# Four more heads' queries and 14 instead of 10 blocks of activations as products of weight parts, with low parts by GpSimd

## The chip, the cores and the metric

The kernel runs on one core of one Trainium2 chip. The metric is the device time of one execution in microseconds (us), median of several runs. Before the change it is 2325.83 us (2325.72 to 2327.22, 3 runs).

## The reference

Two transformer blocks run one after the other on 256 tokens of width 1024, all in float32. The first has two layers, and each ends in a PEER feed-forward, the part that the change touches:

```python
def peer_ffn(x, w_q, sub_keys, u, v):
    """PEER: 8 retrieval heads, product keys, top-16 single-neuron experts per head."""
    ...
    q = (xt @ w_q).reshape(T, PEER_HEADS, 2, PEER_HALF)
    s = jnp.einsum('thcd,hcnd->thcn', q, sub_keys).astype(jnp.float32)
    s1, i1 = lax.top_k(s[:, :, 0], K)
    s2, i2 = lax.top_k(s[:, :, 1], K)
    cand_s = (s1[..., :, None] + s2[..., None, :]).reshape(T, PEER_HEADS, K * K)
    ...
    top_s, top_pos = lax.top_k(cand_s, K)
    ...
    gates = jax.nn.softmax(top_s, axis=-1).astype(x.dtype)
    ...
        act = jax.nn.gelu(jnp.einsum('thkd,td->thk', ub, xb), approximate=False)
```

Each token gets 16 experts per head out of 16384, by two lists of 128 keys. An expert's activation is gelu(u . x), and the result is the sum of v over the chosen experts, times gate and activation.

## The kernel before, in words

The kernel (class Kernel) keeps the activations x in SBUF and their transpose in two parts: xh, the high part in the format float32r, and xl, the rest. Weights come from HBM in loads of 1 MB ([128, 2048], line 248, all issued by SP) and each half of 1024 columns, a block, is cut in the same way by split (line 251): ScalarE writes the high part wh (line 257), VectorE the low part wl = w - wh (line 259). A product is then three: high by high, high by low, low by high (mm3, lines 283 to 288). col_plain (line 345) is the other form: plain float32 without parts, which the profile shows as two products for each one of the code. wh and wl have four buffers each, so a fifth block can't be cut before TensorE has used the first.

peer (line 663) runs once per layer. It computes the activations of all 16384 experts, 128 expert groups of 128, and weighs them with a gate matrix that is zero where an expert isn't chosen. It has three stages.

1. The retrieval (lines 716 to 879). queries (line 758) multiplies x by the query weights of a head, two blocks; scores (line 774) multiplies by the keys; select (line 784) finds the 16 best on VectorE by rounds of MAX8, FIND_INDEX8 and MATCH_REPLACE8, adds the candidates (line 793) and picks again; experts (line 804) works out the chosen experts of four heads on VectorE, once after head 4 and once at the end; line 864 takes the exponential of the gates on ScalarE, after line 863 on VectorE. The results are transposed on TensorE (line 873). Heads 2 and 3 use parts (QSPLIT), the others plain float32. Beside this, u_until (line 700) computes activations ahead, a pair of blocks from one load at a time; in the retrieval in plain float32 from xr, the unsplit transpose: 2 groups after head 6, 4 after head 7 (UA = 2), 10 before the last experts (UB = 10).
2. The gate stage (lines 886 to 942): 16 steps of gate_matrix, in which VectorE builds one-hot matrices A and B (lines 892 to 900) and TensorE multiplies them (line 905); u_until continues between the steps up to 38 of the 40 groups that are computed ahead (LEAD - REST), now with parts.
3. The weighing (lines 943 to 963): the rest of the activations, and the output weights v of all experts.

The program is written in the order of a loop, but a scheduler places the instructions of each engine; each engine then runs its own queue in order and waits on semaphores.

Of the kernel before, what the change touches and what calls it, by code (L numbers as in the profile page):

```python
# [9 lines left out]
F32 = mybir.dt.float32  # L10
# [10 lines left out]
T = 256  # L21
# [8 lines left out]
QSPLIT = (2, 3)  # L30
# [4 lines left out]
# ---------------------------------------------------------------- host layout  # L35
def _plan(widths):
    """Blocks of the given widths, packed into loads of at most GW columns."""
    groups, off = [], 0
    cur = []
    for w in widths:  # L40
        if cur and sum(cur) + w > GW:
            groups.append((off, cur))
            off += P * sum(cur)
            cur = []
        cur.append(w)
    groups.append((off, cur))
    return groups, off + P * sum(cur)
# [13 lines left out]
def _cols(w, n0, n=P):  # L61
    """[K, N] -> [128, K/128 * n]: contraction on partitions, chunk by chunk."""
    k = w.shape[0]
    return w[:, n0:n0 + n].reshape(k // P, P, n).transpose(1, 0, 2).reshape(P, -1)
# [33 lines left out]
def layout(i):  # L98
# [24 lines left out]
    # MLA  # L123
# [12 lines left out]
    # second block  # L136
# [62 lines left out]
# ---------------------------------------------------------------- kernel  # L199
class Kernel:  # L200
# [23 lines left out]
    # -------- weights  # L224
    def places(self, *more):
        """Where loads go from here, besides their own two places: pools, or tiles that are idle."""
# [24 lines left out]
    def split(self, src, w):  # L251
# [7 lines left out]
        nc.vector.tensor_tensor(l[:, :w], src, h[:, :w].bitcast(F32), op=ALU.subtract)  # L259
        return h, l  # L260

    def stream(self, name, width=None, split=True, fine=0):
        """The blocks of a weight, cut into pieces of the given width, as (high, low) or as they are. The first
        loads may be cut into blocks."""
# [18 lines left out]
    def mm3(self, out, a, b, first, last):  # L283
        """out += a.T @ b, both as (high, low)."""
# [5 lines left out]
    def banks(self, nt, nb):  # L290
        """[nt][nb] psum banks of 512 columns."""
        return [[self.mm.tile([P, 512], F32, name="row", tag="mm") for _ in range(nb)] for _ in range(nt)]

    def rows_steps(self, ps, blocks, xT, ks, width=D, hold=0, first=True, last=True, pieces=None):
        """ps[t][n] += x[t, ks] @ W[ks, n], W in blocks of whole rows. The last blocks, as many as held, are taken
        for one token tile after the other, so that the first is done early; the second then by pieces of
        columns, if they are given, with a psum for each."""
# [37 lines left out]
    def col_product(self, out, h, l, xT, nk, c0=0):  # L335
        """out[n, t] = W[:, n].T @ x.T, W as chunks of 128 columns."""
# [5 lines left out]
    def col_plain(self, out, w, x, nk):  # L342
        """The same in plain float32, which needs no parts."""
# [3 lines left out]
    # -------- transposes  # L347
    def turn(self, src, nk, c0=0):
        """x[t, k] of a token tile -> x.T in psum, 4 blocks of 128 in a bank."""
# [9 lines left out]
    def parts(self, banks, t, xT, gain=None, raw=None):  # L359
        """x.T as (high, low), times a gain per k; also as it is if raw is given."""  # L360
# [21 lines left out]
    # -------- norms  # L382
    def bcast(self, ap, n):
        """One row to all partitions."""
# [4 lines left out]
    def table(self, func, after=None):  # L389
        """Brings in the activation table of a function ahead of its use, once the last weight parts (or another  # L390
        [128, 1]) are there."""
# [8 lines left out]
    def ln_residual(self, ps, gb, t):  # L400
        """x = layer_norm(ALPHA * x + ps), one token tile."""
# [16 lines left out]
    def load_gb(self, l, j, pool=None):  # L418
        """Gain and bias of a layer norm, to all partitions."""
# [7 lines left out]
    # -------- log sigmoid of z  # L427
    def log_sigmoid(self, pool, out, z, shape):
# [9 lines left out]
        # what rounding took from 1 + e, over 1 + e to the first order  # L438
# [6 lines left out]
    # -------- mLSTM layer  # L445
    def mlstm(self):
# [3 lines left out]
        with ExitStack() as ctx:  # L450
# [43 lines left out]
            def gates():  # L494
# [13 lines left out]
                # lf in two parts, of which the first sums exactly; B and a in two parts too  # L508
# [89 lines left out]
            def normalise(g):  # L598
                """hs of four heads: y = hs / den, layer norm of y (but for its gain), times the output gate."""
# [9 lines left out]
                for t in range(2):  # L609
# [4 lines left out]
                    # sigmoid(z) = (1 + tanh(z / 2)) / 2  # L614
# [3 lines left out]
            # the output gate, four heads at a time, between the heads' products  # L618
# [33 lines left out]
    def ln_end(self, ps, gb, steps):  # L652
        """The rest of the products for the second token tile, over the layer norm of the first."""
# [8 lines left out]
    # -------- PEER  # L662
    def peer(self, l, ps, gb, banks):
        """ps, gb: psum of the layer before and its norm, which comes first; banks: x.T of its first token tile."""
# [3 lines left out]
        LEAD, KEEP, REST, HALF, UA, UB = 40, 8, 2, 64, 2, 10  # L668
        with ExitStack() as ctx:
            pools = [ctx.enter_context(tc.tile_pool(name=f"pe{j}", bufs=1)) for j in range(4)]  # L670
            pool = pools[3]
            # x waits in DRAM, its place takes loads
            xd = self.dram.tile([P, 2, D], F32, name=f"xd{l}")
            # gate matrices (64 i2 at a time) and activations ahead of their use, one [128, T] slot each
# [25 lines left out]
            def u_until(n, xr=None):  # L700
                """activations of the experts of two i2 at a time."""
                while nu[0] < min(n, P):
# [3 lines left out]
                    for j in range(2):  # L706
                        w = raw[:, j * BW:(j + 1) * BW]
                        if xr is not None:
                            self.col_plain(ps[:, j, :], w, xr, 8)
                        else:  # L710
                            self.col_product(ps[:, j, :], *self.split(w, BW), xT, 8)
# [4 lines left out]
            # retrieval  # L716
            with ExitStack() as c2:
# [4 lines left out]
                def carve(shape):  # L722
                    """float32 scratch in the slots of the first gate matrix."""
# [17 lines left out]
                # places for the first activations past those that come with the retrieval  # L741
# [11 lines left out]
                # The k-th best pair (a, b) of two sorted lists has (a + 1)(b + 1) <= k + 1, and every pair that  # L753
                # dominates it comes before it, so 64 of the 256 pairs hold the best 16, in the same order.
# [3 lines left out]
                def queries(hd, t=None):  # L758
                    """queries of a head, for one token tile or both."""
# [1190 lines left out]
```

## Time and profile before

| | |
|---|---|
| median of 3 runs | 2325.83 us (2325.72 to 2327.22) |
| profiled execution, span from first to last instruction | 2325.0 us |
| TensorE busy | 2284.3 us, 98% |
| VectorE busy | 1597.1 us, 69% |
| ScalarE busy | 1154.6 us, 50% |
| GpSimd busy | 17.2 us, 1% |
| retrieval of the first layer, from the first plain query product to the last transposes | 130.4 to 234.5 us |
| the same of the second layer ends at | 1188.3 us |

The profile names TensorE PE, VectorE DVE, ScalarE ACT, GpSimd POOL and SyncE SP; PEld is TensorE's weight load. A share over the whole span is an average over stages that have different limits, so a stage is read from the busy time in its own stretch and from the wait that ends last in it. The chain that ended last lies on TensorE for the most part; the profile's own list of it gives PE 46% of the span, DVE 2% and ACT 1%. The profiled execution lies within 0.04% of the median.

### The profile page before, as it was taken

How to read it: one execution, taken by the hardware profiler on the slowest of the kernel's cores; microseconds unless marked ns; L12 is line 12 of the kernel's file. 1: busy time of each engine (PE TensorE's matmuls, PEld its weight loads, DVE VectorE, ACT ScalarE, POOL GpSimd, SP SyncE). 2: the span in 40 equal slices, each digit the busy share in tenths (PEclk: the TensorE clock that was granted, in tenths of full speed). 3: DMA queues.
4: the chain of work that ended last, by engine and by line, in shares of the span. 5: the costliest groups of instructions: out<-in, count | busy, mean ns of one | idle time of the engine just before them, and what ended most of it. 6: DMA issues, size and time to landing. Idle time of an engine off the chain costs nothing. (4 is left out here: it accounts for less than half of the span.)

```text
span 2325.0 us, 38721 instructions
## 1 busy us (share of the span) xinstructions
PE 2284.3 (98%) x15802; PEld 2042.5 (88%) x15802; DVE 1597.1 (69%) x2959; ACT 1154.6 (50%) x1773; POOL 17.2 (1%) x41
## 2 busy tenths in 40 slices
PE   8999999999999999999999999999999999999998
PEld 7788998899999999887989889999999988778997
DVE  5789887677555555775998867765555567876555
ACT  5522554555444444574145555554444456466445
POOL 0000000000000000000000000000000000100000
PEclk9999999999999999999999999999999999999999
DMA  7352445545555655444334555455565556516451
GB/s 259 109 218 91 164 146 199 181 165 180 175 188 183 251 187 184 164 170 149 144 130 162 175 188 172 173 177 186 181 247 193 182 204 224 159 37 235 173 190 73
DMA packets 63519, 405.03 MB, mean 174 GB/s; under 512 B 9081, under 2 KB 12006, under 8 KB 17006
## 3 DMA queue, kind: packets, MB, share of 16 engines
q1 hardware_dynamic: 62462, 401.81, 49.2%
q8 instruction: 124, 2.03, 0.4%
q0 software_dynamic: 256, 0.52, 0.1%
q14 instruction: 53, 0.43, 0.1%
q10 hardware_dynamic: 624, 0.23, 0.0%
HBM read 398.48 MB, written 3.54 MB: 173 GB/s over the span
## 5 line engine op out<-in xcount | busy, mean ns | idle before, releaser
L259 DVE TENSOR_TENSOR wl<-raw,wh 128x1024 fp32r<-128x1024 f32 (+2 forms) x519 | 628.1, 1214 | 380.3 <-ACT wh L257 379.2
L257 ACT ACTIVATE wh<-raw 128x1024 fp32r<-128x1024 f32 (+2 forms) x519 | 542.0, 1050 | 476.9 <-PE pu L287 243.7
L286 PE MATMUL pu<-xh,wh 128*128 128x256 f32 x1888 | 537.8, 285 | 0.0
L287 PE MATMUL pu<-xl,wh 128*128 128x256 f32 x1888 | 535.6, 284 | 0.0
L288 PE MATMUL pu<-xh,wl 128*128 128x256 f32 x1888 | 535.4, 284 | 0.0
L286 PE MATMUL row<-wh,whi 128*128 128x512 f32 x1024 | 402.2, 393 | 0.0
L287 PE MATMUL row<-wl,whi 128*128 128x512 f32 x1024 | 399.0, 390 | 0.0
L288 PE MATMUL row<-wh,wlo 128*128 128x512 f32 x1024 | 398.7, 389 | 0.0
L286 PEld LDWEIGHTS pu<-xh,wh 128*128 128x128 f32 x1888 | 363.7, 193 | 3.4
L287 PEld LDWEIGHTS pu<-xl,wh 128*128 128x128 f32 x1888 | 363.5, 193 | 3.4
L288 PEld LDWEIGHTS pu<-xh,wl 128*128 128x128 f32 x1888 | 363.4, 193 | 0.0
L259 DVE TENSOR_TENSOR wl<-x,wh 128x1024 fp32r<-128x1024 f32 x156 | 191.1, 1225 | 133.0 <-ACT wh L257 133.0
L257 ACT ACTIVATE wh<-x 128x1024 fp32r<-128x1024 f32 x156 | 165.0, 1058 | 178.5 <-PE pu L287 126.2
L288 PEld LDWEIGHTS row<-wh,wlo 128*128 128x128 f32 x1024 | 192.2, 188 | 40.8
L286 PEld LDWEIGHTS row<-wh,whi 128*128 128x128 f32 x1024 | 192.6, 188 | 37.3
L287 PEld LDWEIGHTS row<-wl,whi 128*128 128x128 f32 x1024 | 192.6, 188 | 36.7
L924 ACT ACTIVATE whi<-store 128x512 fp32r<-128x512 f32 x128 | 81.1, 634 | 177.1 <-PE row L287 174.3
L925 DVE TENSOR_TENSOR wlo<-store,whi 128x512 fp32r<-128x512 f32 x128 | 88.5, 693 | 74.3 <-ACT whi L924 72.9
L287 PE MATMUL pgu<-xl,wh 128*128 128x256 f32 x352 | 99.7, 283 | 0.0
L288 PE MATMUL pgu<-xh,wl 128*128 128x256 f32 x352 | 99.6, 283 | 0.0
L286 PE MATMUL pgu<-xh,wh 128*128 128x256 f32 x352 | 99.5, 283 | 0.0
L286 PE MATMUL row<-wh,xh 128*128 128x512 f32 (+3 forms) x232 | 87.8, 380 | 1.7 <-ACT xh L370 1.5
(544 smaller groups left out, 3305.7 us busy)
## 6 DMA issues: line engine op xcount, KB each, us to landing
raw<-in_v_dram SPq DMA_DIRECT2D x88, 1024.0 KB, 4.9
raw<-in_u_dram SPq DMA_DIRECT2D x84, 1024.0 KB, 4.9
x<-in_v_dram SPq DMA_DIRECT2D x40, 1024.0 KB, 4.9
x<-in_u_dram SPq DMA_DIRECT2D x38, 1024.0 KB, 4.9
raw<-in_fgu_dram SPq DMA_DIRECT2D x22, 1024.0 KB, 4.8
raw<-in_pg_dram SPq DMA_DIRECT2D x12, 1024.0 KB, 5.4
raw<-in_fdn_dram SPq DMA_DIRECT2D x11, 1024.0 KB, 4.9
store<-in_pq_dram SPq DMA_DIRECT2D x10, 1024.0 KB, 7.3
```

Source lines behind the costliest of these rows:

```text
L257: nc.scalar.activation(h[:, :w], src, AF.Copy)
L259: nc.vector.tensor_tensor(l[:, :w], src, h[:, :w].bitcast(F32), op=ALU.subtract)
L286: mm(out, lhsT=a[0], rhs=b[0], start=first, stop=False)
L287: mm(out, lhsT=a[0], rhs=b[1], start=False, stop=False)
L288: mm(out, lhsT=a[1], rhs=b[0], start=False, stop=last)
L924: nc.scalar.activation(wh, w, AF.Copy)
L925: v.tensor_tensor(wl, w, wh.bitcast(F32), op=ALU.subtract)
```

## The change

Three things change in peer, and one helper. QSPLIT names heads 4 to 7 as well, so that their query weights are cut into parts. The activations in the retrieval are computed from parts, not in plain float32. UA goes from 2 to 3 and UB from 10 to 14, so that 7 pairs of blocks, not 5, are computed in the retrieval; since the gate stage continues up to the same 38 groups, it has 12 pairs, not 14. And split takes an engine for the low part: GpSimd for heads 4 to 7 and the activations of the retrieval, VectorE elsewhere. Comments and docstrings are gone, too, which moves line numbers by one or two.

```diff
-QSPLIT = (2, 3)
+QSPLIT = (2, 3, 4, 5, 6, 7)
...
-    def split(self, src, w):
+    def split(self, src, w, low=None):
...
-        nc.vector.tensor_tensor(l[:, :w], src, h[:, :w].bitcast(F32), op=ALU.subtract)
+        (low or nc.vector).tensor_tensor(l[:, :w], src, h[:, :w].bitcast(F32), op=ALU.subtract)
...
-        LEAD, KEEP, REST, HALF, UA, UB = 40, 8, 2, 64, 2, 10
+        LEAD, KEEP, REST, HALF, UA, UB = 40, 8, 2, 64, 3, 14
...
-            def u_until(n, xr=None):
+            def u_until(n, low=None):
...
-                        if xr is not None:
-                            self.col_plain(ps[:, j, :], w, xr, 8)
-                        else:
-                            self.col_product(ps[:, j, :], *self.split(w, BW), xT, 8)
+                        self.col_product(ps[:, j, :], *self.split(w, BW, low), xT, 8)
...
-                            wq[hd] = [self.split(w, BW) for w in wq[hd]]
+                            wq[hd] = [self.split(w, BW, None if hd < 4 else nc.gpsimd) for w in wq[hd]]
...
-                        u_until(UA * (hd - 5), xr)
+                        u_until(UA * (hd - 5), nc.gpsimd)
...
-                u_until(UB, xr)
+                u_until(UB, nc.gpsimd)
```

Two places show how the queues change. GpSimd's queue, from the first layer's mixer to the second block, before (E is the mixer's mask, kcT belongs to the second block):

```order
L582 AFFINE_SELECT E_641<-E_641 128x128 x2
L582 AFFINE_SELECT E_642<-E_642 128x128 x2
L1482 MEMSET kcT 128x30
L1786 MEMSET gqd 128x1024
L1546 MEMSET rep 128x512
```

and after the change:

```order
L583 AFFINE_SELECT E_641<-E_641 128x128 x2
L583 AFFINE_SELECT E_642<-E_642 128x128 x2
L260 TENSOR_TENSOR wl<-raw,wh 128x1024 x4
L260 TENSOR_TENSOR wl<-store_1267,wh 128x1024 x6
L260 TENSOR_TENSOR wl<-raw,wh 128x1024 x4
L260 TENSOR_TENSOR wl<-store_1267,wh 128x1024 x6
L260 TENSOR_TENSOR wl<-raw,wh 128x1024 x6
L260 TENSOR_TENSOR wl<-store_11305,wh 128x1024 x6
L260 TENSOR_TENSOR wl<-raw,wh 128x1024 x4
L260 TENSOR_TENSOR wl<-store_11305,wh 128x1024 x6
L260 TENSOR_TENSOR wl<-raw,wh 128x1024 x2
L1480 MEMSET kcT 128x30
```

There are 44 new subtractions, 22 in each layer, in a stretch where the queue was empty; raw and store are places of loads.

ScalarE's queue at the end of the first retrieval, before (pu is a product of activations, pS the scores of a head, line 864 the exponential of the gates):

```order
L713 ACTIVATE store_1267<-pu 128x512
L782 ACTIVATE store_1265<-pS_1994 128x512
L713 ACTIVATE store_1267<-pu 128x512
L864 ACT_TABLE_LOAD
L864 ACTIVATE store_1266<-store_1266 128x256
L257 ACTIVATE wh<-raw 128x1024 x2
L713 ACT_TABLE_LOAD
L713 ACTIVATE store_1267<-pu 128x512
L257 ACTIVATE wh<-raw 128x1024 x2
L713 ACTIVATE store_1267<-pu 128x512 x2
```

and after the change:

```order
L258 ACTIVATE wh<-store_1267 128x1024 x2
L711 ACTIVATE store_1267<-pu 128x512
L258 ACTIVATE wh<-store_1267 128x1024
L862 ACT_TABLE_LOAD
L862 ACTIVATE store_1266<-store_1266 128x256
L258 ACTIVATE wh<-store_1267 128x1024
L711 ACT_TABLE_LOAD
L711 ACTIVATE store_1267<-pu 128x512
L258 ACTIVATE wh<-raw 128x1024 x2
L711 ACTIVATE store_1267<-pu 128x512
```

High parts of the retrieval's own activations now stand on both sides of the exponential: 19 of the 22 before it, three behind it (the next high parts of raw belong to the last pair, and the ones after those to the gate stage).

## Rows read from the trace of the kernel before

**Rows 1.** The busy table: busy us (share of the span) and instructions.
```profile
PE 2284.3 (98%) x15802; PEld 2042.5 (88%) x15802; DVE 1597.1 (69%) x2959; ACT 1154.6 (50%) x1773; POOL 17.2 (1%) x41
```
**Rows 2.** Busy us by stretch; columns as in the first line.
```profile
core 0: us, PE busy (x) PEld busy (x) DVE busy (x) ACT busy (x) POOL busy (x), PEclk, DMA share, GB/s
148.00:184.00 36.00, 36.00 (x228) 33.52 (x227) 35.14 (x245) 7.02 (x12) 0.00 (x0) 1.00 0.50 193
...
216.00:235.00 19.00, 12.83 (x61) 10.88 (x60) 18.86 (x73) 7.80 (x11) 0.00 (x0) 0.94 0.15 53
...
235.00:245.00 10.00, 10.00 (x92) 9.96 (x91) 8.00 (x10) 4.17 (x8) 0.00 (x0) 0.77 0.48 198
...
245.00:265.00 20.00, 20.00 (x240) 19.87 (x239) 17.58 (x22) 10.79 (x22) 0.00 (x0) 1.00 0.47 159
...
265.50:272.27 6.77, 6.77 (x82) 6.73 (x81) 5.39 (x7) 3.70 (x8) 0.00 (x0) 1.00 0.45 157
```
**Rows 3.** Timeline, PE, retrieval ends: start us, duration us, [idle before <-releaser].
```profile
234.46 0.90 PE L873 MATMUL pT<-ident,store 128*128 128x128 f32 x3 [5.58 <-DVE store L836]
...
1188.30 0.53 PE L873 MATMUL pT<-ident,store 128*128 128x128 f32 x2 [4.45 <-DVE store L836]
```
**Rows 4.** Timeline, PE: one head as parts, one in plain float32.
```profile
147.59 0.36 PE L286 MATMUL pq<-xh,wh 128*128 128x256 f32 x1
...
153.41 1.06 PE L779 MATMUL pS<-store 128*128 128x128 f32 x8
...
168.75 7.07 PE L345 MATMUL pq<-store,raw 128*128 128x256 f32 x32
175.66 0.61 PE L779 MATMUL pS<-store 128*128 128x128 f32 x4
```
**Rows 5.** Groups of POOL: line, operation, count | busy us, mean ns | idle before.
```profile
L582 POOL TENSOR_SCALAR_AFFINE_SELECT E<-E 128x128 f32<-128x128 f32 x16 | 4.4, 294 | 82.6 <-DVE E L580 82.6
...
L1786 POOL MEMSET gqd<- 128x1024 f32 x1 | 1.0, 952 | 0.0
```
**Rows 6.** Timeline, DVE and POOL, in the second block.
```profile
1979.59 0.48 DVE L1450 SCALAR_TENSOR_TENSOR cacc<-hp,t_cvw,cacc 128x256 f32<-128x256 f32 x1
1979.82 1.04 POOL L1518 TENSOR_TENSOR flat<-dupk,t_cposk 128x240 f32<-128x240 f32 x1 [4.26 <-issue]
...
1980.18 0.95 DVE L1450 SCALAR_TENSOR_TENSOR cacc<-hp,t_cvw,cacc 128x256 f32<-128x256 f32 x1
...
1982.39 0.41 DVE L440 TENSOR_TENSOR ls_d<-ls_d,ls_e 128x256 f32<-128x256 f32 x1
1982.72 1.86 DVE L1450 SCALAR_TENSOR_TENSOR cacc<-hp,t_cvw,cacc 128x256 f32<-128x256 f32 x1
1982.88 0.74 POOL L1518 TENSOR_TENSOR flat<-dupk,t_cposk 128x240 f32<-128x240 f32 x1
1983.57 1.60 POOL L1518 TENSOR_TENSOR flat<-dupv,t_cposv 128x240 f32<-128x240 f32 x2
1984.51 0.94 DVE L442 TENSOR_TENSOR ls_u<-ls_u,ls_d 128x256 f32<-128x256 f32 x1
```
**Rows 7.** Timeline, DVE and POOL, some 20 us later.
```profile
2002.88 1.73 POOL L1801 TENSOR_SCALAR_AFFINE_SELECT gAT<-gAT 128x512 f32<-128x512 f32 x1 [17.71 <-ACT gAT L1800]
2002.90 1.22 DVE L259 TENSOR_TENSOR wl<-raw,wh 128x1024 fp32r<-128x1024 f32 x1
...
2004.93 0.63 POOL L1801 TENSOR_SCALAR_AFFINE_SELECT gAT<-gAT 128x512 f32<-128x512 f32 x1
```
**Rows 8.** Groups of DVE, 148 to 234 us: columns as in rows 5.
```profile
L829 DVE TENSOR_TENSOR oh<-kh,jm 128x1024 f16<-128x1024 f16 x8 | 5.4, 692 | 0.0
...
L793 DVE TENSOR_TENSOR cand<-store 128x32 f32<-128x32 f32 x16 | 2.8, 173 | 0.0
```
**Rows 9.** Timeline, ACT, end of the first retrieval.
```profile
218.42 0.42 ACT L864 ACTIVATE store<-store 128x256 f32<-128x256 f32 x1 [9.46 <-DVE store L863]
218.74 1.99 ACT L257 ACTIVATE wh<-raw 128x1024 fp32r<-128x1024 f32 x2
```

## The prediction

> **What bounds the kernel now.** I read four views. The busy table first [rows 1]: TensorE is busy for 98% of the span, GpSimd for 1%, and GpSimd has 41 instructions in all. Then busy time by stretch [rows 2], for the first of the two retrievals (148 to 235 us) and the gate matrices behind it (245 to 265 us). Two regimes show. In the retrieval VectorE has no hole (35.14 of 36.00 us, then 18.86 of 19.00), while TensorE runs out of work near its end (12.83 of 19.00). In the gate stage it is the other way: TensorE 20.00 of 20.00, VectorE 17.58. The third view, TensorE's waits, names the end of the retrieval [rows 3]: the transposes of line 873 wait 5.58 us for VectorE's last write of line 836, and 4.45 us in the second layer. So the retrieval ends when VectorE's selection ends; every product in it is filler. What TensorE saves there buys nothing by itself. It buys something only as work taken out of the TensorE-bound gate stage. The fourth view is the timeline around the few GpSimd operations that read SBUF beside VectorE [rows 6, 7].
>
> **TensorE's share.** Two blocks in plain float32 take 175.66 - 168.75 = 6.91 us from the first product to what follows; two blocks as three products of parts take 153.41 - 147.59 = 5.82 us [rows 4]. Per layer four heads and five pairs of activations change form: 9 x 1.09 = 9.8 us less. Two more pairs come in (14 instead of 10 blocks): 2 x 5.82 = 11.6 us more. TensorE has 1.8 us more to do in the retrieval, inside its 5.58 us (second layer 4.45) of waiting: price nothing while VectorE ends last.
>
> Those two pairs leave the gate stage. A step there with a pair takes 6.77 us of TensorE and 5.39 of VectorE [rows 2]; now three steps in four have one instead of seven in eight. A step without a pair needs 6.77 - 5.82 = 0.95 of TensorE and, two low parts of 1.22 less [rows 7], 2.95 of VectorE. Four steps: 3 x 6.77 + 0.95 = 21.3 against 3 x 5.39 + 2.95 = 19.1. TensorE still ends last, so all 11.6 us per layer come off, 23.3 us in both. Their two loads of 1 MB per layer move ahead on SP's queue too; the DMA share around the retrieval's end is 0.15 [rows 2], so I cost that at nothing.
>
> **ScalarE.** Twenty-two high parts per layer join a queue that is busy 7.02 of 36 and 7.80 of 19 us [rows 2]; at 1.0 us each (1.99 for two, [rows 9]) there is room. But order counts. The exponential of the gates waits 9.46 us for VectorE's line 863 [rows 9]; in the changed order the high part of the 20th block stands behind it, and with it the last three low parts on GpSimd. If VectorE keeps its time, that is at 218.4 us, TensorE stops for some 2 us, and its slack covers that. If VectorE is late, TensorE is late with it.
>
> **GpSimd, the unknown price.** No row has a subtraction of 128x1024 there. Bounds: the memset of 128x1024, which reads nothing, took 0.95 us; an addition of 128x240 with two inputs took 0.73, which scaled in full is 3.12 us [rows 5, 6]. The addition is the nearest. The selects took 0.29 us for 128 elements and 0.63 for 512 [rows 5, 7], which puts a fixed part at 0.29 - 0.34 / 3 = 0.18; so 0.18 + (0.73 - 0.18) x 1024 / 240 = 2.53 us, an estimate and my value. TensorE wants a block each 2.91 us, so 2.53 keeps up; 3.12 would not quite. GpSimd's queue holds nothing else there (0.00 us busy, [rows 2]), so nothing of before comes to stand behind the new operations.
>
> **What GpSimd does to VectorE.** This decides. Where GpSimd reads SBUF, VectorE's operations with two SBUF inputs stand still [rows 6]. The fused multiply-add of line 1450 takes 0.48 us alone; it took 0.95 when GpSimd's addition of 1979.82 ran, and 1.86 when two additions (1982.88, 1983.57) came one behind the other: it let both pass. The addition of line 442, 0.41 for its like at line 440, took 0.94 beside the third. These three GpSimd operations (0.74 and 1.60 for two) cost VectorE 1.38 + 0.53 = 1.9 us. The reverse is there too: beside a low part on VectorE (1.22 us) a GpSimd select took 1.73 instead of 0.63 [rows 7]. Whoever started first had its way.
>
> The Trainium skill says this as a rule ("SBUF — State Buffer", section "Who interferes with whom"): VectorE's instructions with two SBUF inputs and GpSimd's that read SBUF share an exclusive read interface, and the later one blocks until the earlier has ended. The trace agrees (0.48 became 1.86 us). It speaks against this change; without it the sum would be the second rival's.
>
> VectorE's operations are short (most 0.17 to 0.69 us, [rows 8]) and GpSimd's 2.53 long, so nearly all waiting falls on VectorE. Count it, per layer, for 22 GpSimd operations:
> 1. Selections of heads 0 to 4. Maxima and index searches have one input; only the four candidate additions of a head have two, in two places, so ten encounters. GpSimd works 2 x 2.53 us per head of 6.73 (5.82 + 0.9 for the scores, [rows 4]), a share of 0.75, with 1.27 us left on average: up to 10 x 0.95 = 9.5. The second place of a head comes close behind the first, which often just waited one out, so I take two thirds: 6.
> 2. The experts of heads 0 to 3: almost only two-input work. The four buffers of parts let GpSimd run four blocks ahead of TensorE; 12 low parts are done before and the 20th stands behind the exponential, so seven fall here. Each costs its length less what VectorE's running operation still needs, 2.3 us: 16.
> 3. The experts of heads 4 to 7: the last three, behind the exponential: 7.
>
> Sum 29 us per layer. The retrieval ends 29 later, the gate stage is 11.6 shorter: 17.4 per layer, 35 in both. The span (2325.0) and the median (2325.8) are 0.8 us apart, so 2326 + 35 = **2361 us**. With 0.95 us per GpSimd operation the same count gives 1.3 + 10 x 0.85 = 9.8 per layer and 2322; with 3.12 it gives 11 + 29.5 = 40.5 and 2384, and some 8 more over both layers if GpSimd is then also too slow for TensorE: 2392. TensorE's clock dropped over its wait (granted 0.77 in 235 to 245 us, [rows 2]); that start is paid in both kernels.
>
> The skill also has a time for the operation ("GPSIMD Engine Reference", section 3.1: 4497 ns for a float32 addition of 2048 elements); half of it, an estimate of 2.25 us, would make the sum about 2354. No run here shows that size.
>
> **Rivals.**
> - *GpSimd does the waiting* (2302 us). If VectorE's dense short operations hold GpSimd off, or a large GpSimd operation lets go in between, VectorE keeps its time and 23.3 us come off. For it: in rows 7 GpSimd was the one that waited, and TensorE has slack for it. Against: in rows 6 GpSimd's second addition went ahead of a VectorE operation that already waited.
> - *The waiting is shared* (2332 us): half of 29 is 14.5 per layer, less 11.6, twice. The balance lies at 11.6 us per layer, at about 1.1 us per GpSimd operation.
> - *One-input operations wait as well* (2414 us): then all 22 count, 22 x 2.53 = 55.7, less 11.6, twice 44. For it: nothing shows maxima or index searches beside GpSimd. Against: in rows 6 only two-input operations are stretched.
> - *The change doesn't do what it says*: if the new products starve, TensorE gains nothing in the retrieval, but it has slack there; this joins the forecast's upper end.
>
> **How the numbers follow.** Forecast 0.71 (its own range 2335 to 2392), shared waiting 0.09, GpSimd waits 0.15, one-input operations wait 0.05. A range of 2322 to 2392 leaves out the last two. A measurement of this kernel can tell about 0.2% (4.7 us) from no change. Faster: the 0.15 and a little of the low end, 0.17; same 0.05; slower 0.78.
>
> **What would show it.** Right: in the retrieval, candidate additions and the experts' operations of up to 2.5 us and more on VectorE with GpSimd's subtractions under them; the transposes of line 871 near 263 us, not 234; TensorE idle for some 20 us ahead of the block behind the exponential; two-block groups at 5.82 us; GpSimd busy for 44 x 2.53 = 111 us more. Wrong: VectorE's operations at their old lengths and GpSimd's stretched instead (second reading: the first rival); maxima longer than 0.3 us (the third); GpSimd's subtraction near 1 us or above 3.

## The result, and the profile after

The changed kernel takes 2355.84 us (median of 4 runs, 2355.57 to 2356.48) beside 2325.84 us for the kernel before (2325.72 to 2327.22): a ratio of 1.0128, 95% interval 1.0114 to 1.0143, so 30.0 us slower. The forecast was 2361, with a range of 2322 to 2392. The profiled execution has a span of 2353.9 us, 28.9 more than before, so the traces can be set side by side.

The busy table after the change, which answers to [rows 1]:

```profile
PE 2269.8 (96%) x16090; PEld 2041.9 (87%) x16090; DVE 1644.2 (70%) x2951; ACT 1187.0 (50%) x1809; POOL 125.3 (5%) x85
```

TensorE has 14.5 us less to do, GpSimd 108.1 us more, and VectorE, which lost eight low parts, is busy for 47.1 us more with 8 instructions fewer. Its operations became longer, not more.

Busy time by stretch, with the columns of [rows 2]:

```profile
148.00:184.00 36.00, 35.31 (x298) 35.11 (x297) 35.80 (x216) 16.56 (x22) 24.25 (x10) 1.00 0.64 241
184.00:216.00 32.00, 32.00 (x271) 32.00 (x270) 31.90 (x88) 14.77 (x17) 22.15 (x9) 1.00 0.29 100
216.00:240.00 24.00, 4.11 (x35) 3.90 (x33) 23.97 (x173) 1.03 (x2) 0.00 (x0) 0.64 0.00 0
240.00:255.00 15.00, 11.25 (x73) 10.72 (x73) 14.86 (x32) 8.50 (x11) 7.69 (x3) 0.78 0.20 70
```

VectorE still has no hole. From 184 to 216 it got through 88 instructions, while GpSimd worked 22.15 us; from 216 to 240, with GpSimd at 0.00, it got through 173 in a shorter stretch (the operations of the two stretches differ, so this is a hint and no measure). TensorE stands almost still there (4.11 of 24.00), where before it was short of work only for the last 6 us.

TensorE's longest waits, and where they lie in the first layer, answer to [rows 3]:

```profile
PE pu L287 <- ACT wh L258: 40.6, 2, 20.3
PE pT L871 <- DVE store L834: 10.8, 4, 3.8
```

```profile
240.38 0.58 PE L287 MATMUL pu<-xh,wh 128*128 128x256 f32 x1 [20.28 <-ACT wh L258]
259.40 0.90 PE L871 MATMUL pT<-ident,store 128*128 128x128 f32 x3 [3.75 <-DVE store L834]
```

ScalarE's queue tells why the first of these waits for a high part (beside [rows 9], where the same exponential began at 218.42):

```profile
238.97 0.42 ACT L862 ACTIVATE store<-store 128x256 f32<-128x256 f32 x1 [28.05 <-DVE store L861]
```

The exponential waits for VectorE, the 20th block's high part stands behind it, and TensorE waits for that. The last transposes of the first retrieval begin at 259.40 instead of 234.46, 24.9 us later. The profiled execution after the change has its first scores 1.1 us earlier (145.68 instead of 146.78; it is as much ahead at 35 us, before anything that changed), so counted from there the retrieval is 26.0 us longer. In the second layer the last transposes begin at 1227.61 instead of 1188.30, of which 12.3 come from the first layer (the first scores are late by that much), so 27.0.

Now VectorE beside GpSimd, at the experts of heads 0 to 3 (start us, duration us; GpSimd's rows first):

```profile
191.53 2.41 POOL L260 TENSOR_TENSOR wl<-raw,wh 128x1024 fp32r<-128x1024 f32 x1 [1.35 <-ACT wh L258]
194.42 2.45 POOL L260 TENSOR_TENSOR wl<-raw,wh 128x1024 fp32r<-128x1024 f32 x1 [0.48 <-ACT wh L258]
197.29 2.40 POOL L260 TENSOR_TENSOR wl<-store,wh 128x1024 fp32r<-128x1024 f32 x1 [0.41 <-ACT wh L258]
```

```profile
192.34 0.22 DVE L749 FIND_INDEX8 Q<-store,tmp 128x8 uint32<-128x64 f32 x1
192.48 0.21 DVE L748 MAX8 store<-tmp 128x8 f32<-128x64 f32 x1
192.60 1.42 DVE L812 TENSOR_SCALAR ki<-Q 128x128 uint32<-128x128 uint32 x1
...
194.65 2.37 DVE L815 TENSOR_TENSOR store<-store 128x128 f32<-128x128 f32 x1
...
197.34 2.45 DVE L819 TENSOR_SCALAR store<-store 128x128 f32<-128x128 f32 x1
```

Read the pairs by their ends. The addition of line 815 starts at 194.65 and ends at 197.02, just after GpSimd's subtraction that began at 194.42 and ends at 196.87; alone it takes 0.28. The next subtraction begins at 197.29, and line 819, begun at 197.34, is held until 199.79. The maximum and the index search at 192.3 to 192.7 lie inside a subtraction and keep their 0.2 us. And two of the held operations, lines 812 and 819, have one input: nothing in the rows of before had shown that.

GpSimd's own price, beside the estimate of 2.53 us:

```profile
L260 POOL TENSOR_TENSOR wl<-store,wh 128x1024 fp32r<-128x1024 f32 x24 | 59.1, 2462 | 72.9 <-ACT wh L258 72.9
```

The other 20 have a mean of 2459 ns. Most take 2.40 us. The four longest, 2.82 to 2.85, begin while a VectorE product of 128x1024 (line 827, 0.68 us alone) is under way: there GpSimd is the one that waits, by some 0.4 us, and hardly anywhere else.

### The profile page after: what moved, and what is told of

Read it like the earlier page. It is cut to its first block, busy times and chain, and to the rows that moved or that the text cites. A ratio compares the mean times of both kernels' runs of the same rounds, so it can differ in the third digit from the quotient of the medians.

```text
span 2353.9 us, 39444 instructions
## 1 busy us (share of the span) xinstructions
PE 2269.8 (96%) x16090; PEld 2041.9 (87%) x16090; DVE 1644.2 (70%) x2951; ACT 1187.0 (50%) x1809; POOL 125.3 (5%) x85
## 4 chain that ended last, share of the span: by engine, by line
PE 86%; DVE 11%; ACT 1%; DMA 1%; issue 0%; DVEq 0%; SPq 0%; ACTq 0%
PE row L287 14%; PE row L289 13%; PE row L288 13%; PE pu L287 9%; PE pu L288 9%; PE pu L289 9%; PE pG L903 3%; PE pgu L288 2%; PE pgu L289 2%; PE pgu L287 2%; PE pq L346 1%; DVE tmp L747 1%; DVE wl L260 1%; DVE oh L827 1%; DVE store L745 1%; DVE I L749 1%
## 5 line engine op out<-in xcount | busy, mean ns | idle before, releaser
L260 DVE TENSOR_TENSOR wl<-raw,wh 128x1024 fp32r<-128x1024 f32 (+2 forms) x511 | 617.6, 1213 | 364.6 <-ACT wh L258 363.6
L258 ACT ACTIVATE wh<-raw 128x1024 fp32r<-128x1024 f32 (+2 forms) x531 | 553.9, 1048 | 503.7 <-PE pu L288 241.4
L287 PE MATMUL pu<-xh,wh 128*128 128x256 f32 x2048 | 585.7, 286 | 40.6 <-ACT wh L258 40.6
L289 PE MATMUL pu<-xh,wl 128*128 128x256 f32 x2048 | 583.0, 285 | 3.4 <-POOL wl L260 3.4
L288 PE MATMUL pu<-xl,wh 128*128 128x256 f32 x2048 | 583.1, 285 | 0.0
L287 PEld LDWEIGHTS pu<-xh,wh 128*128 128x128 f32 x2048 | 396.6, 194 | 44.4 <-ACT wh L258 41.0
L289 PEld LDWEIGHTS pu<-xh,wl 128*128 128x128 f32 x2048 | 396.2, 193 | 4.0 <-POOL wl L260 4.0
L288 PEld LDWEIGHTS pu<-xl,wh 128*128 128x128 f32 x2048 | 396.7, 194 | 3.4
L260 POOL TENSOR_TENSOR wl<-raw,wh 128x1024 fp32r<-128x1024 f32 x20 | 49.1, 2459 | 949.0 <-ACT wh L258 949.0
```

What stands on the lines that cost most here:

```text
L258: nc.scalar.activation(h[:, :w], src, AF.Copy)
L260: (low or nc.vector).tensor_tensor(l[:, :w], src, h[:, :w].bitcast(F32), op=ALU.subtract)
L287: mm(out, lhsT=a[0], rhs=b[0], start=first, stop=False)
L288: mm(out, lhsT=a[0], rhs=b[1], start=False, stop=False)
L289: mm(out, lhsT=a[1], rhs=b[0], start=False, stop=last)
```

## The experiments

Two theories stood against each other. Theory A, the prediction's: VectorE's operations wait while GpSimd reads SBUF, and VectorE ends the retrieval. Theory B: GpSimd is harmless, and the loss is the order on ScalarE, where high parts stand behind the exponential; TensorE's two stops of 20.3 us are larger than the whole loss, so the waits alone would name this one.

### Zeros instead of the subtraction

```diff
-        (low or nc.vector).tensor_tensor(l[:, :w], src, h[:, :w].bitcast(F32), op=ALU.subtract)
+        if low is None:
+            nc.vector.tensor_tensor(l[:, :w], src, h[:, :w].bitcast(F32), op=ALU.subtract)
+        else:
+            low.memset(l[:, :w].bitcast(F32), 0.0)
```

> GpSimd fills each of the 44 low parts with zeros instead of subtracting: it writes the same tile at the same place in every queue but reads nothing, and the low part itself is left out of those products. Theory A (VectorE's operations wait while GpSimd reads SBUF): the retrieval ends near its old 234.5 us, the gate stage keeps its 11.6 us per layer of gain, and the time is 2326 - 23 = 2303 us (2299 to 2310). Theory B (the exponential that stands ahead of the last high parts on ScalarE, and the stop of TensorE behind it, makes the loss): the order on ScalarE is the same, so the time stays within 5 us of 2356. Theory C (anything that GpSimd does on SBUF stops VectorE, writes too): by 0.95 us each, the prediction's lower bound, 2322.

Measured: 2299.63 us, ratio 0.9883 (0.9867 to 0.9900), 27.2 us below the 2326.9 of the kernel before beside it. Every queue has the order of the changed kernel. GpSimd's reading is gone, each of its operations is 0.96 us long instead of 2.46, and the time is 56 us shorter; which of the two matters is told by the rows below and by the second probe. Theory B falls, and so does C. GpSimd's writing isn't quite free, though. Its group, its rows, and two of VectorE's rows:

```profile
L263 POOL MEMSET wl<- 128x1024 f32 x44 | 42.2, 958 | 1031.6 <-PE pq L292 986.8 <-PE pu L292 42.0 <-DVE Q L752 2.8
```

```profile
193.04 0.95 POOL L263 MEMSET wl<- 128x1024 f32 x1 [1.92 <-PE pu L292]
195.92 0.96 POOL L263 MEMSET wl<- 128x1024 f32 x1 [1.93 <-PE pu L292]
```

```profile
193.12 1.29 DVE L833 TENSOR_TENSOR oh<-oh,If 128x1024 f16<-128x1024 f16 x2
...
195.94 1.02 DVE L828 CAST If<-I 128x128 f16<-128x128 uint32 x1
```

Two-input operations of line 833 run at their 1.29 us for two right through the fill of 193.04, while the cast of line 828, 0.22 alone, lasts as long as the fill of 195.92. The tensor_scalars that begin at 186.48 and 190.48 are held by fills too (0.94 and 0.72 us instead of 0.23). So a GpSimd operation that only writes holds these one-input operations, and one that reads as well holds two-input ones too.

### The low parts by VectorE

```diff
-        (low or nc.vector).tensor_tensor(l[:, :w], src, h[:, :w].bitcast(F32), op=ALU.subtract)
+        nc.vector.tensor_tensor(l[:, :w], src, h[:, :w].bitcast(F32), op=ALU.subtract)
```

> VectorE makes all low parts; GpSimd has none. Theory A: VectorE is the engine that ends the retrieval, so 22 low parts of 1.22 us at most, less their overlap with the next operation, some 1.15 us each, come on top: 25.3 us per layer later, 11.6 back in the gate stage, 13.7 net, 2326 + 27 = 2353 us (2345 to 2360). GpSimd's help would then have been worth nothing: it costs VectorE as much in waiting as the work itself. Theory B (GpSimd itself is harmless, the order on ScalarE is the loss): 25 us per layer come on top of the changed kernel, about 2400.

Measured: 2350.50 us, ratio 1.0104 (1.0087 to 1.0121). That is 5 us below the changed kernel and 2.5 below the 2353 worked out; B's 2400 is out. VectorE does all 44 low parts here, and the last transpose of the first retrieval starts at 259.9 us, as in the changed kernel: GpSimd's help cost VectorE at least what the work itself would have cost.

### The heads alone, the activations alone

Heads 4 to 7 by GpSimd, with the activations as before (plain float32, UA = 2, UB = 10):

```diff
-        LEAD, KEEP, REST, HALF, UA, UB = 40, 8, 2, 64, 3, 14
+        LEAD, KEEP, REST, HALF, UA, UB = 40, 8, 2, 64, 2, 10
...
-                        self.col_product(ps[:, j, :], *self.split(w, BW, low), xT, 8)
+                        if plain is not None:
+                            self.col_plain(ps[:, j, :], w, plain, 8)
+                        else:
+                            self.col_product(ps[:, j, :], *self.split(w, BW, low), xT, 8)
...
-                u_until(UB, nc.gpsimd)
+                u_until(UB, None, xr)
```

> The query half of the change alone: heads 4 to 7 as parts with low parts by GpSimd (8 subtractions per layer), activations in plain float32 and 10 groups as before. Theory A: these subtractions fall beside the selections, whose maxima and index searches don't wait; the changed kernel lost 4.2 us per layer there in 12 subtractions, so 8 cost some 3 us per layer unless one falls into the experts' stretch (2.2 us each then), and nothing is gained in the gate stage: 2326 + 6 = 2332 us (2328 to 2338). Theory B: ScalarE's order around the exponential is as before, so 2326 within 2.

The activations by GpSimd, with heads 4 to 7 in plain float32:

```diff
-QSPLIT = (2, 3, 4, 5, 6, 7)
+QSPLIT = (2, 3)
```

> The activations' half alone: 14 groups as parts with low parts by GpSimd (14 subtractions per layer), heads 4 to 7 in plain float32. Theory A: these stand at the experts' stretches, where nearly every VectorE operation has two inputs; 7 and 3 of them waited there in the changed kernel, 20.7 us per layer, less 11.6 in the gate stage, 9.1 twice: 2344 us, and up to 2354 if more of the 14 fall there, now that none are done in the heads before (range 2340 to 2358). So this half carries most of the loss. Theory B (order on ScalarE): the same order around the exponential as in the changed kernel, about 2350: this run doesn't tell A from B.

Measured: heads alone 2330.42 us, ratio 1.0017 (1.0007 to 1.0026); activations alone 2348.68 us, ratio 1.0093 (1.0076 to 1.0110). Both lie where theory A put them. The heads alone hardly tell the theories apart (3.5 us over, interval 1.6 to 6.0, where B allowed 2); their rows do. In the heads' run two candidate additions of the first layer are held, 2.30 and 0.66 us instead of 0.17 and 0.20: 2.6 us for eight subtractions. TensorE's saving went nowhere:

```profile
PE pT L874 <- DVE store L837: 20.7, 6, 4.7
```

It waits 20.7 us at the two ends instead of some 10.6. In the activations' run the last four subtractions of the first retrieval fall into the experts of heads 4 to 7, and three of the four operations that they hold have one input:

```profile
238.81 2.32 DVE L815 TENSOR_TENSOR store<-store 128x128 f32<-128x128 f32 x1
241.38 2.07 DVE L816 CAST kh<-store 128x128 f16<-128x128 f32 x1
243.37 2.43 DVE L817 TENSOR_SCALAR store<-store 128x128 f32<-128x128 f32 x1
245.72 2.45 DVE L819 TENSOR_SCALAR store<-store 128x128 f32<-128x128 f32 x1
```

A GpSimd subtraction costs VectorE 0.3 to 0.5 us on average beside a selection and some 2.1 beside the experts; where it falls decides.

### The exponential behind the high parts

```diff
-        nc.scalar.activation(h[:, :w], src, AF.Copy)
+        self.cut = nc.scalar.activation(h[:, :w], src, AF.Copy).ins
...
                 u_until(UB, nc.gpsimd)
+                cut = self.cut
                 experts(1)
...
-                nc.scalar.activation(G8, G8, AF.Exp)
+                with tc.issue_after(cut):
+                    nc.scalar.activation(G8, G8, AF.Exp)
```

> The changed kernel with the exponential of the gates queued on ScalarE behind the last high part of the retrieval, so that no high part waits for VectorE's line 861. Theory A (VectorE waits for GpSimd): TensorE's 20-us stop ahead of the block behind the exponential goes, but it was only where TensorE waited for VectorE, and that it does for as long at the transposes now. The three low parts leave the last experts' stretch (6.4 us per layer there) and go ahead of it, where some of them fall beside the experts of heads 0 to 3 and some beside selections: 0 to 5 us per layer less than the changed kernel, 2346 to 2356. Theory B (the order is the loss): 20.3 us of stop per layer come back, 2356 - 41 = 2315 us.

Measured: 2356.85 us, ratio 1.0134 (1.0118 to 1.0149): the changed kernel's time, 0.9 us over A's upper end and 42 over B's. The stop didn't go, it moved to the transposes of the results (timeline of TensorE):

```profile
251.35 0.45 PE L873 MATMUL pT<-ident,store 128*128 128x128 f32 x1 [22.41 <-DVE store L834]
...
258.59 1.11 PE L873 MATMUL pT<-ident,store 128*128 128x128 f32 x3 [2.28 <-DVE store L834]
```

With a third wait of 3.82 between them (at 255.62) that is 28.5 us of waiting against 20.3 + 1.7 + 5.7 before the edit, and the last transposes start at 258.59 instead of 259.40. The three low parts that left the last experts' stretch came down on the first one: two products of line 830 take 5.70 us there instead of 1.29, six operations of line 833 3.63 instead of 1.43.

```profile
213.21 5.70 DVE L830 TENSOR_TENSOR oh<-oh,If 128x1024 f16<-128x1024 f16 x2
218.83 3.63 DVE L833 TENSOR_TENSOR oh<-oh 128x512 f16<-128x512 f16 x6
```

### Ten groups, not fourteen

```diff
-        LEAD, KEEP, REST, HALF, UA, UB = 40, 8, 2, 64, 3, 14
+        LEAD, KEEP, REST, HALF, UA, UB = 40, 8, 2, 64, 2, 10
```

> The changed kernel with 10 groups in the retrieval, as before the change, not 14 (UA = 2): 18 GpSimd subtractions per layer, and nothing moved out of the gate stage. Tells the gain term by itself. By the prediction's steps: the gate stage gives nothing back (11.6 us per layer lost against the changed kernel), and four GpSimd subtractions fewer per layer give back 0.35 us each if they fall beside selections and 2.1 each if beside experts (1.4 to 8.4): 3 to 10 us per layer above the changed kernel, 2356 + 6 to 20 = 2362 to 2376 us. If the gate stage's gain were not real (TensorE bound elsewhere), it would be below 2356.

Measured: 2368.39 us, ratio 1.0182 (1.0166 to 1.0198), 12.6 us above the changed kernel. So the two pairs moved out of the gate stage are a real gain: without them the time rises, though there are eight subtractions fewer. If the pairs are worth the 11.3 us per layer that the traces of before and after show in the mean (below), the eight subtractions take off 2 x 11.3 - 12.6 = 10.0 us, 1.3 each, between the price beside a selection and the price beside the experts. That is a rough price, since the order of VectorE's own low parts at the end differs in the two kernels, too.

### Twelve groups in plain float32, nothing on GpSimd

```diff
-        LEAD, KEEP, REST, HALF, UA, UB = 40, 8, 2, 64, 2, 10
+        LEAD, KEEP, REST, HALF, UA, UB = 40, 8, 2, 64, 2, 12
```

(against the kernel before)

> The kernel before with one thing from the change: 12 groups of activations in the retrieval, not 10, in plain float32 as before, nothing on GpSimd. TensorE had 5.58 and 4.45 us of waiting at the ends of the two retrievals. One more pair in plain float32 is 6.91 us there (1.3 and 2.5 us beyond the waiting) and takes 5.82 out of the gate stage: 4.5 + 3.4 = 7.8 us less, 2326 - 8 = 2318 us (2316 to 2322). If the pair collides with something else at the end of the retrieval (its load, or its table change on ScalarE), no gain: 2326.

Measured: 2314.10 us, ratio 0.9951 (0.9938 to 0.9965): faster than both, by 11.7 us where 7.8 were worked out. TensorE's timeline at the end of the first retrieval has no wait left, and in the second layer none either:

```profile
233.04 0.82 PE L874 MATMUL pT<-ident,store 128*128 128x128 f32 x6
```

The trace's gain is larger than worked out in both layers: from the first scores to the first product with output weights the first layer is 7.8 us shorter (192.8 before, 185.0 here; 4.5 worked out), the second with what follows 5.1 (3.4). What the sum left out is TensorE's clock. The 5.6 us behind the last transposes, in the kernel before and in this one:

```profile
234.40:240.00 5.60, 5.54 (x28) 5.54 (x29) 5.60 (x8) 1.09 (x2) 0.00 (x0) 0.53 0.89 360
```

```profile
233.00:238.60 5.60, 5.60 (x48) 5.56 (x47) 5.37 (x7) 3.12 (x5) 0.00 (x0) 1.00 0.93 364
```

With its wait of 5.58 us behind it, TensorE had the lower of its two levels (1.2 of 2.4 GHz) for most of the stretch (granted 0.53 in the mean) and did 28 matmuls; with work up to the end it kept 1.00 and did 48. Twenty matmuls at 0.12 us are 2.4 us that the wait cost on top of itself. In the second layer, behind the wait of 4.45 us, the same length has a granted 0.70 and 34 matmuls against 1.00 and 48: 1.7 us. The sum of 7.8 with 2.4 and 1.7 is 11.9, beside 7.8 + 5.1 = 12.9 in the traces and 11.7 between the medians. (The first experiment points the same way: it waited 3.4 us, had a granted 0.94 from 235 to 245 us where [rows 2] show 0.77, and came out 3.4 us below the 2303 that left the clock out.)

### Which operations wait, by themselves

Two runs put a probe behind the finished output of the kernel before. In the first, ten kinds of VectorE operation ran beside 24 subtractions of GpSimd:

> Behind the kernel before, once its output is written, GpSimd makes 24 subtractions of 128x1024, one about every 3 us (each is fed by three copies on ScalarE), while VectorE runs ten each of ten kinds of operation on 128x128: MAX8, FIND_INDEX8, MATCH_REPLACE8, a reduction, TENSOR_SCALAR (contiguous, and with a stride of two elements), a cast to float16, a copy out of PSUM, a subtraction with one input in PSUM, one with both in SBUF. The time is longer by some 80 us and means nothing else. Theory A as predicted (only operations with two inputs in SBUF wait): only the last kind takes over 1 us beside GpSimd. Theory A2, after what the changed kernel's experts showed: the TENSOR_SCALARs wait too, up to 2.3 us, perhaps the cast; MAX8, FIND_INDEX8, MATCH_REPLACE8 and whatever reads PSUM do not.

GpSimd's subtractions came in pairs with pauses of 4 us, and all TENSOR_SCALARs but one fell into a pause, so their question stayed open. It did show casts of 2.24 and 2.18 us, two-input subtractions of 2.37 and 2.23, and index searches, replacements, copies out of PSUM and subtractions with one input in PSUM at 0.27 to 0.28 inside GpSimd's work. MAX8 and the reduction ran before GpSimd began. The second probe settles the rest:

```python
for kind in kinds:
    for f in (lambda: v.tensor_tensor(tt, s, s1, op=ALU.subtract), kind, kind):
        with tc.issue_after(last.ins):
            last = f()
```

> The probe again, since GpSimd's pauses in the first one left some kinds untouched: now 44 subtractions of GpSimd back to back behind the kernel before, and on VectorE, in a fixed order, one subtraction with both inputs in SBUF (it waits, so it ends as GpSimd begins its next one) and then two of a kind, for thirteen kinds. The time itself means nothing. Theory A (only two SBUF inputs wait): of the kinds only the float16 addition takes over 1 us. Theory A2 (from the experts' stretch and the first probe's cast of 2.24 us): also the three TENSOR_SCALARs out of SBUF and both casts, 1.9 to 2.3 us each, while MAX8, FIND_INDEX8, MATCH_REPLACE8, the reduction and what has an input in PSUM keep 0.2 to 0.3 us. If VectorE never gets in between GpSimd's back-to-back operations, the first subtraction shows one wait of 100 us.

Its groups on VectorE (count | busy us, mean ns), beside one row of GpSimd:

```profile
L1978 DVE TENSOR_TENSOR tt<-px 128x128 f32<-128x128 f32 x13 | 27.8, 2137 | 0.0
L1975 DVE TENSOR_TENSOR h<-h 128x128 f16<-128x128 f16 x2 | 4.6, 2318 | 0.0
L1971 DVE CAST cf<-u 128x128 f32<-128x128 uint32 x2 | 4.6, 2316 | 0.0
L1968 DVE TENSOR_SCALAR tq<-px 128x128 f32<-128x128 f32 x2 | 4.6, 2315 | 0.0
L1969 DVE TENSOR_SCALAR u<-u 128x128 uint32<-128x128 uint32 x2 | 4.6, 2315 | 0.0
L1970 DVE CAST c<-px 128x128 f16<-128x128 f32 x2 | 4.6, 2314 | 0.0
L1967 DVE TENSOR_SCALAR ts<-px 128x128 f32<-128x128 f32 x2 | 4.6, 2314 | 0.0
...
L1963 DVE MAX8 m<-px 128x8 f32<-128x128 f32 x2 | 0.6, 288 | 0.0
L1972 DVE COPY cp<-pm 128x128 f32<-128x128 f32 x2 | 0.6, 284 | 0.0
L1973 DVE TENSOR_SCALAR tm<-pm 128x128 f32<-128x128 f32 x2 | 0.6, 284 | 0.0
L1974 DVE TENSOR_TENSOR tp<-pm,px 128x128 f32<-128x128 f32 x2 | 0.6, 283 | 0.0
L1964 DVE FIND_INDEX8 i<-m,px 128x8 uint32<-128x128 f32 x2 | 0.6, 282 | 0.0
L1966 DVE TENSOR_REDUCE rd<-px 128x1 f32<-128x128 f32 x2 | 0.6, 279 | 0.0
L1965 DVE MATCH_REPLACE8 rp<-m,px 128x128 f32<-128x128 f32 x2 | 0.5, 273 | 0.0
```

```profile
2328.16 101.95 POOL L1958 TENSOR_TENSOR pl<-px,ph 128x1024 fp32r<-128x1024 f32 x44 [302.42 <-ACT ph L1957]
```

There is no middle. The upper seven are held until a GpSimd subtraction ends, 2.31 us where they begin with it; the lower seven take 0.29 us or less (pm is in PSUM, all else in SBUF; the operation on tq reads and writes with a stride of two elements). Theory A2 holds as put. Line 1973 against line 1967 is the cleanest pair: the same operation, once out of PSUM and once out of SBUF. And GpSimd loses next to nothing by them: 101.95 / 44 = 2.32 us each, and its last ones, beside which VectorE does nothing, begin 2.30 us apart.

## Why the prediction was right, point by point

**What ends the retrieval.** VectorE, in both kernels and in the experiments but two: with the plain twelve groups the two end together, and with ten groups one last transpose (257.37 us) stands behind products in TensorE's queue, 2.5 us after VectorE's last write. That TensorE's share buys nothing there was right: the heads alone turned it into 10 us more waiting.

**The gate stage, 11.6 us per layer.** From the last transposes to the first product with output weights in the first layer the changed kernel is 11.9 us shorter (24.9 late, then 13.0 late), in the second 10.7: 11.3 in the mean. The ten-group run agrees that the moved pairs carry it.

**ScalarE's order.** As forecast: three low parts behind the exponential, TensorE idle for 20.28 us ahead of the block. Not a cause of its own, as the third and the first experiment show.

**GpSimd's price.** 2.53 us estimated, 2.40 for most and 2.46 in the mean: the scaling of the addition of 128x240 was 3% to 5% high. The estimate of 2.25 us worked out from the Trainium skill ("GPSIMD Engine Reference", section 3.1) was as far off on the other side; the 2.32 us back to back in the probe is the nearest that a run comes to it. GpSimd was busy for 108 us more, beside 111.

**The three places of waiting.** Per layer the prediction had 6 + 16 + 7 = 29 us. Summing what each held operation of the first layer takes over its usual length gives 4.2 for the candidate additions, 17.1 for the experts of heads 0 to 3 (eight operations held by a subtraction each, and 0.7 of a cast), and 6.4 for the last three: 27.7; the same sum for the second layer gives 29.1. Over both layers VectorE's busy time says the same: 47.1 us more, although 8 low parts of 1.14 us were taken off it, is 56 us, 28 per layer.

So the count was good, but one of its rules was not. I had taken one-input operations as free. Selections are, since their maxima, index searches and replacements are; the experts' shifts, scalings and casts are not, and three of the eight operations held in the first experts are of that kind. The count came out because I let all seven subtractions meet something there anyway, and because errors offset: 1.8 too much for the first place, 1.1 too little for the second, 0.6 too much for the third. That much of the agreement is luck. The Trainium skill has the missing half in the very section that the prediction cites ("SBUF — State Buffer", "Who interferes with whom"): copies, casts and tensor_scalar can run in a mode that takes both ports, and then contend, reductions don't. The Trainium skill's page "VectorE: DVE Perf Modes" (section "Mode 2×_2P — use both read ports for one tensor") confines that to one source and to SBUF. The probe agrees in every row that these pages speak of, 2.31 us out of SBUF and 0.28 out of PSUM, and so does the fill of the first experiment, which held a cast and let two-input products run.

**The step that was mis-sized.** 29 - 11.6 = 17.4 per layer were forecast; the span grew by 28.9, 14.5 per layer. Of the 2.9 us per layer between, most is an order that the prediction didn't look at: it took the waiting alone for what makes the retrieval longer. In the kernel before three of VectorE's low parts for the gate stage stand ahead of its last write of line 836 and one behind; after the change one stands ahead and three behind (one row for the three). VectorE's timeline before and after:

```profile
230.44 1.22 DVE L259 TENSOR_TENSOR wl<-raw,wh 128x1024 fp32r<-128x1024 f32 x1
...
231.78 1.22 DVE L259 TENSOR_TENSOR wl<-raw,wh 128x1024 fp32r<-128x1024 f32 x1
...
233.05 1.22 DVE L259 TENSOR_TENSOR wl<-raw,wh 128x1024 fp32r<-128x1024 f32 x1
234.18 0.22 DVE L836 TENSOR_TENSOR store<-oh 128x64 f32<-128x64 f16 x1
234.32 1.22 DVE L259 TENSOR_TENSOR wl<-raw,wh 128x1024 fp32r<-128x1024 f32 x1
```

```profile
258.00 1.22 DVE L260 TENSOR_TENSOR wl<-raw,wh 128x1024 fp32r<-128x1024 f32 x1
259.13 0.22 DVE L834 TENSOR_TENSOR store<-oh 128x64 f32<-128x64 f16 x1
259.27 3.49 DVE L260 TENSOR_TENSOR wl<-raw,wh 128x1024 fp32r<-128x1024 f32 x3
```

Two low parts at 1.14 us, 2.3 per layer, left the path: 27.7 - 2.3 = 25.4, beside 26.0 measured for the first retrieval, and 29.1 - 2.3 = 26.8, beside 27.0 for the second. In the mean of the layers the waits are 28.4, 0.6 less than forecast, and the gate stage gives 0.3 less: 28.4 - 2.3 - 11.3 = 14.8, beside 14.5. The order of the two kernels could have told this beforehand.

**Slips.** The prediction says that without the shared interface the sum would be the second rival's; it would be the first's (2302), and the first experiment gave 2299.6. "Whoever started first had its way" doesn't come out of its rows: in [rows 7] the select that waited has the earlier start (2002.88 against 2002.90), and in [rows 6] the multiply-add of 1982.72 waited for the addition of 1982.88. And the bounds of the range took 1.3 and 11 us for the first place; by the rule that gave 6 (two thirds of the encounters) they are 0.9 and 9.6, which moves the ends by 1 and 3 us.

**The rivals.** GpSimd does the waiting: GpSimd's subtractions vary by 0.5 us, VectorE's operations become up to 2.2 us longer. Shared waiting: fell with it. All one-input operations wait: fell for selections (maxima 0.28 us as before), where twelve subtractions would have cost some 2.2 us each instead of 4.2 in all, 22 us more per layer; true for tensor_scalar and casts.

**The clock.** "That start is paid in both kernels" was right for this comparison: in the 5.6 us behind the last transposes of the two layers the changed kernel has a granted 0.61 and 0.50, the kernel before 0.53 and 0.70. It was too short as a lesson: the plain twelve groups show that the start was worth 2.4 and 1.7 us, and could be had back.

## What to carry to other kernels

An engine's idle time is no price list: before work goes to an idle GpSimd, list what VectorE runs at that time and which of it has two inputs in SBUF or is a copy, cast or tensor_scalar from SBUF, since each of these that meets a GpSimd operation is held for the rest of it; beside rounds of MAX8 and FIND_INDEX8 the help is cheap (0.3 to 0.5 us for a subtraction), beside dense elementwise work it costs more (2.1 us) than VectorE needs for the work itself (1.14 us). The longest wait in a table (here TensorE's 20.3 us for ScalarE) may only be the last link behind a late engine: move it, and see whether it comes back elsewhere. A short wait of TensorE can cost some 0.4 of itself again in clock (2.4 us after 5.58, 1.7 after 4.45), so filling it with one more block, even in a dearer form, may be worth more than making the fill cheaper.

## What the runs showed of the hardware

- Beside a GpSimd operation with SBUF inputs, VectorE's tensor_scalar (contiguous or with a stride of two), casts and float16 or float32 two-input operations out of SBUF are held until GpSimd's ends (2.31 us where they begin with it, instead of 0.22 to 0.28); MAX8, FIND_INDEX8, MATCH_REPLACE8, reductions and whatever takes an input from PSUM keep 0.27 to 0.29 us.
- Beside a GpSimd fill, which reads nothing, a cast and a tensor_scalar are held (1.02 us instead of 0.22, 0.94 instead of 0.23) and a two-input product is not (1.29 for two).
- With GpSimd's operations back to back, a held VectorE operation still gets in after one of them (two tensor_scalars held one after the other take 4.6 us, against GpSimd's 2.32 each). In [rows 6] one seemed to let two shorter GpSimd operations pass; why that differs was not tried.
- After 5.58 us of waiting TensorE's clock was granted at 0.53 over the next 5.6 us, at a cost of 20 matmuls of 0.12 us; after 4.45 us at 0.70, at a cost of 14.
